# Two panels of a mixer's input product as 512-wide matmuls over high and low parts side by side

## The chip, the core and the metric

The kernel runs on one core of a Trainium2 chip. The metric is the device time of one execution in microseconds. The core has five engines that run their own instruction streams and wait for each other through semaphores: TensorE (PE; its weight loads are listed as PEld), VectorE (DVE), ScalarE (ACT), GpSimd (POOL) and SyncE (SP), which issues the loads here. Matmuls write into PSUM, which has 8 banks of 128 partitions by 512 float32 values; ACT and DVE read them out.

## What is computed

One layer of a hybrid decoder trunk over 256 tokens of width 2048. The part that matters here is the start: a norm, the input product, and the token shift of three of its outputs.

```python
h = rms_norm(x, attn_norm[i])
z = h @ w_in[0]
z_pool = z[..., :POOL_WIDTH]
zs = token_shift(z[..., POOL_WIDTH:IN_WIDTH], mu_shift[i])
...
def token_shift(z, mu):
    zf = z.astype(jnp.float32)
    z_prev = jnp.pad(zf, ((0, 0), (1, 0), (0, 0)))[:, :-1]
    return zf + (z_prev - zf) * mu.astype(jnp.float32)
```

The shifted r, k and v (1024 columns each) feed an RWKV-7 time mixing in two groups of 8 heads; the pooled part feeds a causal pooling; both join in an output product. A squared-ReLU MLP, a gated embedding and a last norm follow.

## The kernel before

Everything is float32, and a product is made of three products of a faster type, float32r. A weight W is split into a high part (an ACT copy into float32r) and a low part (a DVE subtraction), and so is the activation x; W x is taken as Wh xh + Wh xl + Wl xh.

**Stages.** The mixer runs from the start to about 370 us, the MLP after it, then the gate and the last norm. At the start x, transposed, is loaded by k-tile (128 of the 2048 features by 256 tokens), and a small product for the decay, gate and learning-rate inputs runs on it (`wag`). Meanwhile the norm's factor is found. `normed` multiplies each k-tile by it (a DVE product, L438) and splits the result (L176 on ACT, L177 on DVE) into the high tiles `hTh` and the low tiles `hTl`, two tiles each of 8 k-tiles.

**Panels.** The input weights come as panels of 512 columns. `gemm_cols` makes one panel: for each of 8 loads (two k-tiles by 512 columns, split at L171 and L172) and each half of the panel it runs the two column tiles of 128 over both k-tiles, three products of 256 columns each (L184 to L186). The result stands with features on partitions and tokens along the row, two column tiles in one bank, so a panel needs two banks. `z_product` makes such a panel and evacuates each half as soon as it is done: ACT scales it by 1 - mu into SBUF (L487), DVE adds mu times the bank, shifted by a token (L489). The panels are, in order, zk and zr of head group 0, zk and zr of group 1, two of zv, and two of the pooled part, which run in the other orientation.

**Banks.** A ring of three banks (`mm`), one bank apart (`own`) and four for the recurrent work (`rw`) are the 8. zk takes two of the ring, zr one of the ring and `own`, the next zk two of the ring again, so a panel begins in banks that the one before it did not hold.

**Order.** PE's order is written out by hand. The panels are generators in a queue; `fill(us)` runs as many of their steps as their yielded estimates (0.36 us a step) make up, `finish(p)` runs one panel to its end, and between these stand the small products of the recurrent part: the decay and rate products (`rwkv_lora`, L548), the sums and spreads for the key norm (`rwkv_k`, banks `kkn` and `rnb`), the scores (`rwkv_scores`, L640). DVE, ACT, POOL and SP are put in order by a list scheduler with priorities. In `rwkv_k` the keys' norm goes through a root on ACT (L578), a reciprocal (L579) and a spread on PE; DVE then makes the normed keys (L587) and the operands of the scores in tiles `BK` (L606, L607) and `AR` (L608, L611 and, with zr, L616). `make_bands` builds the pooling bands in tile `wband`, on POOL (L133 to L135) and DVE (L136 to L138); this tile takes the place of the norm factor's row, so it waits for the last use of that row in L438.

Of the kernel before, what the change touches and what calls it, by code (L numbers as in the profile page):

```python
# [9 lines left out]
F32 = mybir.dt.float32  # L10
F32R = mybir.dt.float32r
# [5 lines left out]
T = 256  # L17
# [23 lines left out]
def trunk(  # L41
# [43 lines left out]
    def own_bank(name):  # L85
        return psf.tile([128, 512], F32, tag="own", name=name)
# [110 lines left out]
    def gemm_cols(src, acts, name, consume, own=False):  # L197
# [3 lines left out]
        for kp in range(nkp):  # L201
            raw = load_raw(src[kp].rearrange("p a n -> p (a n)"), 1024, f"{name}_{kp}")
            parts = split_w(raw, f"{name}_{kp}")
            for half in range(2):
# [6 lines left out]
                if kp == nkp - 1:  # L211
                    consume(half, banks[half])

    def gemm_toks(src, acts, name, consume, kps=None, hooks=(), banks=None, begin=True, end=True, split_ends=False):
# [54 lines left out]
    def queued(gen):  # L269
        queue.append(gen)  # L270
        return gen
# [5 lines left out]
    def a8(slot, name, dt=F32):  # L277
        return act.tile([128, 2048], dt, tag=f"a{slot}", name=name)
# [27 lines left out]
        nc.vector.reciprocal(rs, rs)  # L306
        return rs

    hT_h = [a8(2 + i, f"hTh{i}", F32R) for i in range(2)]
    hT_l = [a8(4 + i, f"hTl{i}", F32R) for i in range(2)]  # L310

    def hT(k):
        o = (k % 8) * T
        return hT_h[k // 8][:, o : o + T], hT_l[k // 8][:, o : o + T]
# [18 lines left out]
    def flat(t_):  # L333
        return t_.rearrange("p a t -> p (a t)")
# [97 lines left out]
    def normed(*groups):  # L432

        with tc.high_priority(20000):
            xs, hs = [], []
            for k0, n in groups:
                xh = xg[k0 // 4][:, k0 % 4 : k0 % 4 + n]
                nc.vector.tensor_tensor(xh, xh, s_bc.unsqueeze(1).to_broadcast([128, n, T]), op=ALU.mult)  # L438
                xs.append(flat(xh))
                hs.append((k0 // 8, slice(k0 % 8 * T, (k0 % 8 + n) * T)))  # L440
            for x_, (i, o) in zip(xs, hs):
                split_sb(hT_h[i][:, o], hT_l[i][:, o], x_)

    with tc.manual_schedule(engines={mybir.EngineType.DVE}):
        normed((0, 1), (1, 1))
# [25 lines left out]
        nc.scalar.activation(zf[32:64, 2, :], zf[0:32, 2, :], AF.Copy)  # L471


    def z_product(i, tag, mu_name, gi, own):

        box = []

        def consume(half, bank):
            if not box:
                box.append(e4(tag))  # L480
            dst = box[0]
            with tc.high_priority(30000):
                evacs = []
                for p in (2 * half, 2 * half + 1):
                    c = PARAM_COLS[mu_name] - m0 + 4 * gi + p
                    evacs.append((dst[:, p, :], bank[:, p % 2 * T : (p % 2 + 1) * T], col(mu_name, 4 * gi + p)))
                    nc.scalar.activation(evacs[-1][0], evacs[-1][1], AF.Copy, scale=omu[:, c : c + 1])  # L487
                for d_, s_, mu_ in evacs:
                    nc.vector.scalar_tensor_tensor(  # L489
                        d_[:, 1:T], s_[:, 0 : T - 1], mu_, d_[:, 1:T], op0=ALU.mult, op1=ALU.add  # L490
                    )

        return box, queued(gemm_cols(w_in[i + gi], hT, f"{tag}{gi}", consume, own))

    def pair_tile(tag, name, **kw):
# [1133 lines left out]
```

## Time and profile before

| | us |
|---|---|
| median of 3 runs (1162.97 to 1163.73) | 1163.5 |
| the profiled execution | 1163.34 |
| its span | 1161.6 |
| panels zk and zr of group 0 on PE, from the first product to the next panel's | 22.92 to 74.09 |
| first scores product of group 0 | 82.46 |
| clock granted to TensorE, mean | 0.998 |

In the rows of a timeline the first number is the start in microseconds from the start of the span, the second the time covered, then engine, line, operation, output and inputs by the program's names, shapes and count; in square brackets stands how long the engine was idle before it and what it waited for. Matmuls overlap, so the distance between two starts is what one costs, not its duration. The rows of groups give the busy time in us and the mean of one in ns behind the bar.

### The profile page before, as it was taken

What the parts mean: (1) busy time and instruction counts of PE and PEld (TensorE: products, weight loads), DVE (VectorE), ACT (ScalarE), POOL (GpSimd) and SP (SyncE); (2) the same over time, 40 slices, a digit from 0 to 9 for tenths busy, and PEclk for the clock granted to TensorE, in tenths of its full rate; (3) what the DMA queues carried; (4) which work ended last, traced back from release to release, by engine and by line L of the source; (5) the groups of instructions that cost most, each with busy time, mean ns of one, the idle gap of its engine ahead of it and who ended that gap; (6) DMA issues with size and microseconds to landing.
All of it is one profiled execution on the core that took longest, in us unless ns stands there. A gap on an engine that the chain in (4) does not pass through costs nothing.

```text
span 1161.6 us, 19313 instructions
## 1 busy us (share of the span) xinstructions
PE 1150.8 (99%) x7348; PEld 989.2 (85%) x7348; DVE 920.6 (79%) x1223; ACT 689.1 (59%) x1220; POOL 17.2 (1%) x77
## 2 busy tenths in 40 slices
PE   9999999999999999999999999999999999999997
PEld 8999998788888888888888888888888888888886
DVE  7886898356676788888989888888878989888843
ACT  5868555667544655555665755555556665669733
POOL 4100000000000000000000000000000000000000
PEclk9999999999999999999999999999999999999999
DMA  7553544453898999985787887998885778996812
GB/s 274 164 171 127 160 151 152 147 165 109 319 328 277 325 342 343 326 327 191 257 291 250 319 298 280 350 332 328 317 302 180 262 266 287 335 327 227 301 36 73
DMA packets 78445, 290.87 MB, mean 250 GB/s; under 512 B 8720, under 2 KB 9744, under 8 KB 74128
## 3 DMA queue, kind: packets, MB, share of 16 engines
q1 hardware_dynamic: 78064, 289.28, 70.8%
q8 instruction: 57, 0.93, 0.3%
q10 hardware_dynamic: 288, 0.37, 0.1%
q14 instruction: 36, 0.29, 0.1%
HBM read 259.20 MB, written 30.41 MB: 249 GB/s over the span
## 4 chain that ended last, share of the span: by engine, by line
PE 96%; DVE 1%; DMA 1%; ACT 1%; issue 0%; DVEq 0%; ACTq 0%; SPq 0%
PE u_w L1135 21%; PE d_p L1239 15%; PE u_w L1140 10%; PE d_w L1239 9%; PE d_d L1239 3%; PE o_b L193 2%; PE o_b L195 2%; PE o_b L194 2%; PE gt_b L193 2%; PE gt_b L195 2%; PE gt_b L194 2%; PE zp_b L193 2%; PE wag_b L380 1%; PE zr_b L184 1%; PE zk_b L184 1%; PE zk_b L185 1%
## 5 line engine op out<-in xcount | busy, mean ns | idle before, releaser
L1135 PE MATMUL u_w<-h,wh_u 128*128 128x512 f32 x1024 | 321.9, 395 | 0.0
L1140 PEld LDWEIGHTS u_w<-h,wl_u 128*128 128x128 f32 x1024 | 192.4, 188 | 45.4
L171 ACT ACTIVATE wh_u<-raw_u 128x512 fp32r<-128x512 f32 x256 | 147.2, 623 | 133.9 <-PE u_w L1135 99.8
L1140 PE MATMUL u_w<-h,wl_u 128*128 128x256 f32 x1024 | 201.4, 278 | 0.0
L172 DVE TENSOR_TENSOR wl_u<-raw_u,wh_u 128x1024 fp32r<-128x1024 f32 x128 | 156.1, 1220 | 38.1 <-PE u_w L1140 22.6
L1135 PEld LDWEIGHTS u_w<-h,wh_u 128*128 128x128 f32 x1024 | 156.1, 189 | 0.1
L1299 ACT ACTIVATE th_d<-raw_d 128x1024 fp32r<-128x1024 f32 x52 | 52.6, 1053 | 63.1 <-DVE raw_d L1295 43.7
L1239 PE MATMUL d_p<-wh_d,yd 128*128 128x512 f32 x288 | 77.0, 389 | 0.0
L1301 DVE TENSOR_TENSOR tl_d<-raw_d,th_d 128x1024 fp32r<-128x1024 f32 x52 | 61.4, 1221 | 12.4 <-ACT th_d L1299 12.3
L172 DVE TENSOR_TENSOR wl_o<-raw_o,wh_o 128x1024 fp32r<-128x1024 f32 x32 | 39.0, 1223 | 31.3 <-ACT wh_o L171 15.9
L1239 PEld LDWEIGHTS d_p<-wh_d,yd 128*128 128x128 f32 x288 | 54.0, 188 | 11.3
L1239 PE MATMUL d_w<-th_d,ys 128*128 128x512 f32 x240 | 61.5, 390 | 0.0
L171 ACT ACTIVATE wh_o<-raw_o 128x512 fp32r<-128x512 f32 x64 | 36.7, 623 | 40.2 <-PE o_b L194 21.7
L171 ACT ACTIVATE wh_d<-raw_d 128x512 fp32r<-128x512 f32 x96 | 53.9, 619 | 7.0 <-DMA raw_d<-in_w_ffn_down_dram 2.7
L172 DVE TENSOR_TENSOR wl_d<-raw_d,wh_d 128x1024 fp32r<-128x1024 f32 x48 | 57.1, 1217 | 0.0
L1288 ACT ACTIVATE w7h_d<-raw_d 128x1024 fp32r<-128x1024 f32 x40 | 42.2, 1056 | 22.1 <-DMA raw_d<-in_w_ffn_down_dram 8.4
L1239 PEld LDWEIGHTS d_w<-th_d,ys 128*128 128x128 f32 x240 | 44.7, 188 | 9.6 <-ACT th_d L1299 0.5
L1290 DVE TENSOR_TENSOR w7l_d<-raw_d,w7h_d 128x1024 fp32r<-128x1024 f32 x40 | 48.8, 1219 | 4.4 <-PE d_d L1239 2.0
L1239 PE MATMUL d_p<-w7h_d,ys 128*128 128x512 f32 x160 | 49.3, 389 | 0.0
L1239 PE MATMUL d_p<-wl_d,yd 128*128 128x512 f32 x144 | 44.3, 389 | 0.0
L1289 ACT ACTIVATE w7h_d<-raw_d 128x512 fp32r<-128x512 f32 x40 | 25.0, 624 | 24.4 <-PE d_d L1239 19.5
L172 DVE TENSOR_TENSOR wl_zp<-raw_zp,wh_zp 128x1024 fp32r<-128x1024 f32 x16 | 19.5, 1223 | 24.6 <-ACT wh_zp L171 24.6
(390 smaller groups left out, 2694.5 us busy)
## 6 DMA issues: line engine op xcount, KB each, us to landing
raw_u<-in_w_ffn_up_dram SPq DMA_DIRECT2D x128, 512.0 KB, 6.3
raw_d<-in_w_ffn_down_dram SPq DMA_DIRECT2D x106, 512.0 KB, 5.9
raw_ta<-in_w_ffn_down_dram SPq DMA_DIRECT2D x44, 512.0 KB, 6.8
tad<-ta SPq DMA_DIRECT2D x22, 1024.0 KB, 5.7
raw_o<-in_w_out_dram SPq DMA_DIRECT2D x32, 512.0 KB, 5.2
tr_d<-tad SPq DMA_DIRECT2D x28, 512.0 KB, 5.1
raw_gt<-in_w_ple_gate_dram SPq DMA_DIRECT2D x24, 512.0 KB, 4.6
raw_zk<-in_w_in_dram SPq DMA_DIRECT2D x16, 512.0 KB, 3.5
```

The lines of the kernel that those rows point to most:

```text
L171: nc.scalar.activation(wh[:, a * 512 : (a + 1) * 512], raw[:, a * 512 : (a + 1) * 512], AF.Copy)
L172: nc.vector.tensor_tensor(wl, raw, wh.bitcast(F32), op=ALU.subtract)
L193: nc.tensor.matmul(o, a_h, wh[:, 0:n], start=first, stop=False)
L194: nc.tensor.matmul(o, a_l, wh[:, 0:n], start=False, stop=False)
L195: nc.tensor.matmul(o, a_h, wl[:, 0:n], start=False, stop=last)
L1135: nc.tensor.matmul(bank[:, ct, :].rearrange("p (s t) -> p s t", s=2), wh[:, c], hl, start=k == 0, stop=False, skip_group_check=True,)
L1140: nc.tensor.matmul(bank[:, ct, 0:T], wl[:, c], hl[:, 0, :], start=False, stop=k == 15, skip_group_check=True)
L1239: nc.tensor.matmul(o, l, r, start=first, stop=last, skip_group_check=True)
L1288: nc.scalar.activation(ha, ra, AF.Copy)
L1290: nc.vector.tensor_tensor(la, ra, ha.bitcast(F32), op=ALU.subtract)
L1299: nc.scalar.activation(th[:, r], tr[r], AF.Copy)
L1301: nc.vector.tensor_tensor(tl[:, r], tr[r], th[:, r].bitcast(F32), op=ALU.subtract)
```

## The change

The first two panels, zk and zr of head group 0, are made in another way; the six others stay. The high and low part of a normed k-tile now lie side by side in one tile (`hTq`, four tiles of 4 k-tiles each, in the same places), so that one product of the high weights runs over 512 columns: Wh times xh and Wh times xl land in the two halves of a bank. The low weights add their 256 columns onto the first half. A column tile thus fills a bank, and a panel holds four: the whole ring and `own`. Both panels do. To evacuate a tile, ACT copies the second half of the bank, DVE adds the first half to it in a tile `zs`, and the two shift instructions then read `zs` in place of the bank. `zs` lies in the ring of two that the scores' tile uses. A step now covers two column tiles and yields 0.7.

```diff
+    def gemm_cols_wide(src, name, consume):
+        banks = [mm_bank(f"{name}_b{i}") for i in range(3)] + [own_bank(f"{name}_b3")]
...
+            for half in range(2):
+                cts = (2 * half, 2 * half + 1)
+                for a, (wh, wl) in enumerate(parts):
+                    k = 2 * kp + a
+                    hl = hTq[k // 4][:, k % 4]
+                    for ct in cts:
+                        nc.tensor.matmul(
+                            banks[ct].rearrange("p (s t) -> p s t", s=2), wh[:, ct * 128 : (ct + 1) * 128], hl,
+                            start=k == 0, stop=False, skip_group_check=True,
+                        )
+                    for ct in cts:
+                        nc.tensor.matmul(
+                            banks[ct][:, 0:T], wl[:, ct * 128 : (ct + 1) * 128], hl[:, 0],
+                            start=False, stop=k == 2 * nkp - 1, skip_group_check=True,
+                        )
+                    yield 0.7
+                if kp == nkp - 1:
+                    consume(half, [banks[ct] for ct in cts])
...
-    hT_h = [a8(2 + i, f"hTh{i}", F32R) for i in range(2)]
-    hT_l = [a8(4 + i, f"hTl{i}", F32R) for i in range(2)]
+    hTq = [a8(2 + i, f"hT{i}", F32R).rearrange("p (k s t) -> p k s t", k=4, s=2) for i in range(4)]
...
+        def consume_wide(half, banks):
...
+                for p, b in zip(ps, banks):
+                    nc.scalar.activation(zs[:, p], b[:, T : 2 * T], AF.Copy)
+                for p, b in zip(ps, banks):
+                    nc.vector.tensor_tensor(zs[:, p], b[:, 0:T], zs[:, p], op=ALU.add)
+                for p in ps:
+                    nc.scalar.activation(dst[:, p], zs[:, p], AF.Copy, scale=omu[:, c : c + 1])
+                for p in ps:
+                    nc.vector.scalar_tensor_tensor(
+                        dst[:, p, 1:T], zs[:, p, 0 : T - 1], col(mu_name, 4 * gi + p), dst[:, p, 1:T], op0=ALU.mult, op1=ALU.add
+                    )
...
-    zk0, p_zk0 = z_product(4, "zk", "mu_k", 0, False)
-    zr0, p_zr0 = z_product(2, "zr", "mu_r", 0, True)
+    zk0, p_zk0 = z_product(4, "zk", "mu_k", 0, False, True)
+    zr0, p_zr0 = z_product(2, "zr", "mu_r", 0, True, True)
```

The scheduled engines get another order around these panels. First DVE while panel zk ends: the norm's last products and the splits of zk's last loads, then the bands. Of before:

```order
L438 TENSOR_TENSOR tD_t<-tD_t,s_bc 128x512
L339 SCALAR_TENSOR_TENSOR zf<-wagT,par_sb,zf 128x255
L172 TENSOR_TENSOR wl_zk_6_566<-raw_zk_6_563,wh_zk_6_565 128x1024
L177 TENSOR_TENSOR hTl_158<-tD_t,hTh_156 128x512
L438 TENSOR_TENSOR tD_t<-tD_t,s_bc 128x512
L172 TENSOR_TENSOR wl_zk_7_597<-raw_zk_7_594,wh_zk_7_596 128x1024
L177 TENSOR_TENSOR hTl_158<-tD_t,hTh_156 128x512
L136 TENSOR_TENSOR wband<-wband,ident 128x128 x2
```

The same place of the change (its lines lie 25 further down, L463 is the norm product):

```order
L463 TENSOR_TENSOR tD_t<-tD_t,s_bc 128x512
L364 SCALAR_TENSOR_TENSOR zf<-wagT_396,par_sb,zf 32x255
L177 TENSOR_TENSOR hT_158<-tD_t,hT_158 128x2x256
L463 TENSOR_TENSOR tD_t<-tD_t,s_bc 128x512
L172 TENSOR_TENSOR wl_zk_6_520<-raw_zk_6_517,wh_zk_6_519 128x1024
L177 TENSOR_TENSOR hT_158<-tD_t,hT_158 128x2x256
L172 TENSOR_TENSOR wl_zk_7_543<-raw_zk_7_540,wh_zk_7_542 128x1024
L364 SCALAR_TENSOR_TENSOR zf<-wagT,par_sb,zf 128x255
L136 TENSOR_TENSOR wband<-wband,ident 128x128 x2
```

The last norm product moved ahead of the sixth low split. Behind the bands, DVE evacuates zk; there the change has an add for each column tile, `zszk`, ahead of the shifts. Next, DVE from the key norm to the normed keys, of before:

```order
L577 TENSOR_SCALAR rn_860<-kkn 128x32
L594 TENSOR_TENSOR tE_t<-tE_t,zk_t 128x1024
L579 RECIPROCAL rn_860<-rn_860 128x32
L172 TENSOR_TENSOR wl_zr_7_987<-raw_zr_7_984,wh_zr_7_986 128x1024
L580 TENSOR_TENSOR rnq_861<-rn_860,qmask 128x256
L607 TENSOR_TENSOR BK_946<-tE_t,tC_t 128x16x64
L172 TENSOR_TENSOR wl_zk_0_1034<-raw_zk_0_1031,wh_zk_0_1033 128x1024
L587 SCALAR_TENSOR_TENSOR tB_t<-zk_t,par_sb,rnb_928 128x256
```

And of the change, where L623, L625, L640, L626, L653 and L633 are these lines in the same order of work:

```order
L623 TENSOR_SCALAR rn_786<-kkn 128x32
L172 TENSOR_TENSOR wl_zr_7_830<-raw_zr_7_827,wh_zr_7_829 128x1024
L625 RECIPROCAL rn_786<-rn_786 128x32
L640 TENSOR_TENSOR tE_t<-tE_t,zk_t 128x1024
L626 TENSOR_TENSOR rnq_787<-rn_786,qmask 128x256
L172 TENSOR_TENSOR wl_zk_0_928<-raw_zk_0_925,wh_zk_0_927 128x1024
L653 TENSOR_TENSOR BK_856<-tE_t,tC_t 128x16x64
L172 TENSOR_TENSOR wl_zk_1_959<-raw_zk_1_956,wh_zk_1_958 128x1024
L633 SCALAR_TENSOR_TENSOR tB_t<-zk_t,par_sb,rnb_838 128x256
```

zr's last low split now stands ahead of the reciprocal, and the second split of the next panel ahead of the normed keys; on ACT, zr's last high split has moved ahead of the norm's root. Last, DVE from zr's evacuation to the last operand of the scores, of before:

```order
L172 TENSOR_TENSOR wl_zk_1_1065<-raw_zk_1_1062,wh_zk_1_1064 128x1024
L489 SCALAR_TENSOR_TENSOR zr_t<-zr_b_634,par_sb,zr_t 128x255 x2
L489 SCALAR_TENSOR_TENSOR zr_t<-zr_b_635,par_sb,zr_t 128x255 x2
L172 TENSOR_TENSOR wl_zk_2_1096<-raw_zk_2_1093,wh_zk_2_1095 128x1024
L606 TENSOR_TENSOR BK_946<-tF_t,tC_t 128x16x64
L172 TENSOR_TENSOR wl_zk_3_1140<-raw_zk_3_1137,wh_zk_3_1139 128x1024
L611 TENSOR_SCALAR AR_945<-tB_t 128x16
L616 TENSOR_TENSOR AR_945<-zr_t,tA_t 128x16x64
L172 TENSOR_TENSOR wl_zk_4_1183<-raw_zk_4_1180,wh_zk_4_1182 128x1024
```

Of the change, without the first two adds, which stand just before it, and L605's successor between them:

```order
L533 SCALAR_TENSOR_TENSOR zr_t<-zszr_893,par_sb,zr_t 128x255 x2
L528 TENSOR_TENSOR zszr_893<-zr_b_583,zszr_893 128x256
L528 TENSOR_TENSOR zszr_893<-zr_b_584,zszr_893 128x256
L172 TENSOR_TENSOR wl_zk_2_990<-raw_zk_2_987,wh_zk_2_989 128x1024
L533 SCALAR_TENSOR_TENSOR zr_t<-zszr_893,par_sb,zr_t 128x255 x2
L172 TENSOR_TENSOR wl_zk_3_1034<-raw_zk_3_1031,wh_zk_3_1033 128x1024
L652 TENSOR_TENSOR BK_856<-tF_t,tC_t 128x16x64
L172 TENSOR_TENSOR wl_zk_4_1077<-raw_zk_4_1074,wh_zk_4_1076 128x1024
L654 SCALAR_TENSOR_TENSOR AR_855<-tB_t,tA_t 128x16x63
L657 TENSOR_SCALAR AR_855<-tB_t 128x16
L662 TENSOR_TENSOR AR_855<-zr_t,tA_t 128x16x64
```

The adds are new, and zk's fourth low split now stands ahead of the last operand instead of behind it.

More of the change, by code (lines that the diff above doesn't have):

```diff
@@ L212, in gemm_cols @@
                     consume(half, banks[half])
+    def gemm_cols_wide(src, name, consume):
+        banks = [mm_bank(f"{name}_b{i}") for i in range(3)] + [own_bank(f"{name}_b3")]
+        nkp = src.shape[0]
+        for kp in range(nkp):
+            raw = load_raw(src[kp].rearrange("p a n -> p (a n)"), 1024, f"{name}_{kp}")
+            parts = split_w(raw, f"{name}_{kp}")
+            for half in range(2):
[16 more added lines that the diff above has]
+                    consume(half, [banks[ct] for ct in cts])
     def gemm_toks(src, acts, name, consume, kps=None, hooks=(), banks=None, begin=True, end=True, split_ends=False):
@@ L307, in rms_inv @@
         return rs
-    hT_h = [a8(2 + i, f"hTh{i}", F32R) for i in range(2)]
-    hT_l = [a8(4 + i, f"hTl{i}", F32R) for i in range(2)]
+    hTq = [a8(2 + i, f"hT{i}", F32R).rearrange("p (k s t) -> p k s t", k=4, s=2) for i in range(4)]
     def hT(k):
-        o = (k % 8) * T
-        return hT_h[k // 8][:, o : o + T], hT_l[k // 8][:, o : o + T]
+        hl = hTq[k // 4][:, k % 4]
+        return hl[:, 0], hl[:, 1]
     rp = rctx.enter_context(tc.tile_pool(name="rp", bufs=1))
@@ L438, in normed @@
                 nc.vector.tensor_tensor(xh, xh, s_bc.unsqueeze(1).to_broadcast([128, n, T]), op=ALU.mult)
[L439 to L442, printed above, removed]
+                xs.append(xh)
+                hs.append(hTq[k0 // 4][:, k0 % 4 : k0 % 4 + n])
+            for x_, hl in zip(xs, hs):
+                split_sb(hl[:, :, 0], hl[:, :, 1], x_)
     with tc.manual_schedule(engines={mybir.EngineType.DVE}):
@@ L471, in wag_out, with z_product @@
         nc.scalar.activation(zf[32:64, 2, :], zf[0:32, 2, :], AF.Copy)
-    def z_product(i, tag, mu_name, gi, own):
+    def z_product(i, tag, mu_name, gi, own, wide=False):
         box = []
@@ L491, in consume @@
                     )
+        def consume_wide(half, banks):
+            if not box:
+                box.append(e4(tag))
+                box.append(rp.tile([128, 4, T], F32, tag="SC", bufs=2, name=f"zs{tag}{gi}"))
+            dst, zs = box
+            ps = (2 * half, 2 * half + 1)
+            with tc.high_priority(30000):
+                for p, b in zip(ps, banks):
[3 more added lines that the diff above has]
+                for p in ps:
+                    c = PARAM_COLS[mu_name] - m0 + 4 * gi + p
+                    nc.scalar.activation(dst[:, p], zs[:, p], AF.Copy, scale=omu[:, c : c + 1])
[3 more added lines that the diff above has]
+                    )
+        if wide:
+            return box, queued(gemm_cols_wide(w_in[i + gi], f"{tag}{gi}", consume_wide))
         return box, queued(gemm_cols(w_in[i + gi], hT, f"{tag}{gi}", consume, own))
```

## The prediction

> **What bounds the kernel now.** First the page: busy time of each engine, then the chain that ended last. Then the windows over the stage that the change touches (columns: stretch, its length, PE, PEld, DVE, ACT, POOL busy with counts, granted clock, DMA share, GB/s).
>
> ```profile
> PE 1150.8 (99%) x7348; PEld 989.2 (85%) x7348; DVE 920.6 (79%) x1223; ACT 689.1 (59%) x1220; POOL 17.2 (1%) x77
> PE 96%; DVE 1%; DMA 1%; ACT 1%; issue 0%; DVEq 0%; ACTq 0%; SPq 0%
> 54.00:60.00 6.00, 6.00 (x52) 6.00 (x51) 2.50 (x3) 5.97 (x12) 0.00 (x0) 1.00 0.40 119
> 60.00:66.00 6.00, 6.00 (x109) 5.83 (x108) 2.81 (x5) 5.97 (x12) 0.00 (x0) 1.00 0.59 179
> 66.00:72.00 6.00, 6.00 (x53) 5.54 (x53) 6.00 (x9) 2.87 (x7) 0.00 (x0) 1.00 0.49 167
> 72.00:78.00 6.00, 6.00 (x52) 6.00 (x52) 5.97 (x10) 4.17 (x9) 0.00 (x0) 1.00 0.41 124
> 78.00:84.00 6.00, 6.00 (x57) 5.75 (x57) 6.00 (x8) 2.36 (x7) 0.00 (x0) 1.00 0.68 211
> PE zp_b L195 <- DVE wl_zp L172: 0.3, 1, 0.3
> ```
>
> TensorE is the bound: 99% busy, 96% of the chain, clock 1.00. So a shorter instruction stream on PE shortens the kernel, if nobody becomes late. But between 54 and 66 us ACT has 11.94 of 12 us taken, and between 66 and 84 us DVE has 17.97 of 18. The last row, from the list of waits, is PE's only listed wait inside the mixer after its start, 0.3 us near 191 us: hardly anything later could give lost time back.
>
> **What the wide product saves.** Durations of overlapping matmuls say little; the distance between starts counts. The timeline of PE, first inside the old panel zr, then in the MLP's up product, which has the wide form already:
>
> ```profile
> 59.78 0.28 PE L184 MATMUL zr_b<-hTh,wh_zr 128*128 128x256 f32 x1
> ...
> 60.14 0.28 PE L184 MATMUL zr_b<-hTh,wh_zr 128*128 128x256 f32 x1
> 420.19 0.63 PE L1135 MATMUL u_w<-h,wh_u 128*128 128x512 f32 x2
> ...
> 422.28 0.63 PE L1135 MATMUL u_w<-h,wh_u 128*128 128x512 f32 x2
> ```
>
> Old: three products of 256 columns from 59.78 to 60.14, 0.36 us for one k-tile and column tile. New: from 420.19 to 422.28 lie three rounds of two wide and two narrow products, 2.09/6 = 0.348 us. Two panels have 2x16x4 = 128 such pairs: 128 x 0.012 = **1.5 us saved** on PE, half in each panel. That is little, because a step of 256 costs 0.12 us and one of 512 about 0.227: joining two saves only what each start costs over its columns. The Trainium skill (TensorE: Matmul & The Clock Gate, "Back-to-back issue gap") puts that fixed part at 2.5 ns for an isolated product when warm; 128 of them would be an estimate of 0.3 us instead of 1.5. The rows above speak against it here.
>
> **What it adds.** Each of the 8 column tiles gets one ACT copy of the low half and one DVE add before the old two instructions. The nearest rows are the old evacuations, given by groups with operands and shape: the ACT copy out of PSUM, and the DVE product with one operand in PSUM.
>
> ```profile
> L487 ACT ACTIVATE zr_t<-zr_b,omu 128x256 f32<-128x256 f32 x4 | 1.7, 465 | 0.4 <-PE zr_b L186 0.4
> L587 DVE SCALAR_TENSOR_TENSOR tB_t<-zk_t,par_sb,rnb 128x256 f32<-128x256 f32 x4 | 1.6, 473 | 0.0
> ```
>
> Back to back four take about 1.6 us, 0.39 each, so the four adds of a panel are 1.6 us on DVE. They could cost PE nothing, if DVE has room, or 3.2 us, if both panels' adds hit PE; the place decides. There are three places.
>
> **Place A, panel zk to panel zr.** Before, zr had banks of its own. Now it needs zk's four, and each is free only after its add. PE reaches zr at 46.82 - 64x0.012 = 46.05, plus 0.1 for the first k-tile, whose low part must now be there at once: 46.15. The engines there (timeline):
>
> ```profile
> 40.39 0.69 DVE L438 TENSOR_TENSOR tD_t<-tD_t,s_bc 128x512 f32<-128x512 f32 x1
> 41.23 0.38 POOL L133 MEMSET wband<- 128x144 f32 x2 [22.02 <-DVE tD_t L438]
> 44.79 0.38 DVE L136 TENSOR_TENSOR wband<-wband,ident 128x128 f32<-128x128 f32 x1 [0.74 <-POOL wband L135]
> 46.82 0.28 PE L184 MATMUL zr_b<-hTh,wh_zr 128*128 128x256 f32 x1
> 48.75 1.65 DVE L489 SCALAR_TENSOR_TENSOR zk_t<-zk_b,par_sb,zk_t 128x255 f32<-128x255 f32 x4
> 50.15 0.48 PE L548 MATMUL lw<-zf,wa 64*128 64x256 f32 x1
> 51.38 0.82 ACT L551 ACTIVATE tA_t<-lw,par_sb 128x256 f32<-128x256 f32 x2
> ```
>
> Before, DVE came to zk's evacuation only at 48.75, because it built the bands first and waited for POOL, which waited for the last norm product (40.39). Nobody minded. In the new order this product stands before the sixth low split, so POOL starts some 2 to 3 us earlier and its waits on DVE go; the adds then start between 46.1 and 48.75. I take 46.9. First add done at 47.3: PE waits 1.2 us, and 0.5 more for the second bank and the second half: **1.7 us**. Bounds: 0 (adds before 45.7) and 3.2 (first add from 48.75).
>
> Behind this wait stands the lora product (50.15). The fill ahead of it is now 5 units of two pairs, 3.5 us: 46.15+1.7+3.5 = 51.35, and ACT, which read it at 51.38, can start at 51.85. So ACT's full stretch up to 66 us shifts by 0.45.
>
> **Places B and C, panel zk of the second head group, and the scores.** DVE's queue from the key norm to the scores, with PE's arrivals:
>
> ```profile
> 63.41 1.28 ACT L570 ACT_TABLE_LOAD   x1
> 65.79 0.21 ACT L578 ACTIVATE rn<-rn 128x32 f32<-128x32 f32 x1
> 65.91 1.14 ACT L171 ACTIVATE wh_zr<-raw_zr 128x512 fp32r<-128x512 f32 x2
> 65.92 1.23 DVE L594 TENSOR_TENSOR tE_t<-tE_t,zk_t 128x1024 f32<-128x1024 f32 x1 [1.17 <-ACT tE_t L591]
> 67.06 0.35 DVE L579 RECIPROCAL rn<-rn 128x32 f32<-128x32 f32 x1
> 67.33 1.16 DVE L172 TENSOR_TENSOR wl_zr<-raw_zr,wh_zr 128x1024 fp32r<-128x1024 f32 x1
> 68.41 0.41 DVE L580 TENSOR_TENSOR rnq<-rn,qmask 128x256 f32<-128x256 f32 x1
> 68.73 1.22 DVE L607 TENSOR_TENSOR BK<-tE_t,tC_t 128x1024 f32<-128x1024 f32 x1
> 69.87 1.22 DVE L172 TENSOR_TENSOR wl_zk<-raw_zk,wh_zk 128x1024 fp32r<-128x1024 f32 x1
> 71.00 1.65 DVE L587 SCALAR_TENSOR_TENSOR tB_t<-zk_t,par_sb,rnb 128x256 f32<-128x256 f32 x4
> 74.09 0.28 PE L184 MATMUL zk_b<-hTh,wh_zk 128*128 128x256 f32 x1
> 81.14 1.22 DVE L616 TENSOR_TENSOR AR<-zr_t,tA_t 128x1024 f32<-128x1024 f32 x1
> 82.46 0.49 PE L640 MATMUL sc<-AR,BK 64*128 64x128 f32 x4
> ```
>
> The product at L616 ends at 82.36 and the scores start at 82.46: no slack at all. Whatever DVE loses before it, PE loses too. A whole panel-sized operation takes 1.14 us of DVE (68.73 to 69.87). In the new order ACT splits zr's last high part (1.14) ahead of the norm's root, and DVE does its low part, one low split more (zk1) and later another (zk4) ahead of the scores. Worked through: table load at 63.41+0.45 = 63.86, done with the small copy behind it at 65.3; high split to 66.5; DVE from 66.6: low split 1.14, reciprocal 0.27, L594 1.14, L580 0.32, then low split, L607, low split 3.4, so the normed keys (L587) start at 72.9 and the first add at 74.45, done at 74.9.
>
> B: PE reaches zk1 at 74.09 - 1.5 + 0.1 + 1.7 = 74.4, and its first bank is zr's first one: **0.5 us** (0 to 1.5, as A and DVE fall). C: from 74.45 DVE has four adds 1.6, L605 1.1, four shifts 1.6, three low splits and L606 4.6, L608 and L611 1.2, L616 1.2: 11.3, so 85.75, scores at 85.85. PE would be there at 74.9+8.4 = 83.3: **2.5 us** (0 to 3.5).
>
> Sum: -1.5 + 0.1 + 1.7 + 0.5 + 2.5 = **+3.3 us**. The same from one place: scores at 85.85 instead of 82.46. The other edits cost nothing: the norm's outputs written in steps of two k-tiles have the same sizes; zr's ACT copies lie in waits of ACT (it is at 4.17 of 6 us between 72 and 78; without that cover they would add 1.6), zk's before its full stretch begins; the loads keep their sizes, and DMA is at half. The profiled execution took 1163.34 us (span 1161.6 and 1.7 around it), 0.16 under the median of the runs: 1163.34+3.3 = **1166.6**.
>
> **Rivals.**
> *Banks and DVE keep up* (ends on the other side): if the adds find DVE free, only the shorter stream is left: 1163.34 - 1.4 = 1161.9. For it: DVE is busy 5.3 of 12 us between 54 and 66. Against: the scores' zero slack. It decides where L616 ends before 81.1. The Trainium skill (Perfetto Trace Analysis, "Matmuls") has both sides in one place: larger matmuls are more efficient, and independent groups should rotate through different banks so that evacuation overlaps; the first would give this rival, the second is what the change gives up. Chance 0.08.
> *Only the adds count*: ACT gets to the root in time and the splits taken forward hide in DVE's shorter queue behind; L616 is late by zr's four adds alone, 82.36+1.6 = 83.95, scores 1.6 late: 1164.9. For it: ACT's order depends on when buffers come free. Chance 0.22.
> *Place A is full*: DVE still comes at 48.75, A is 3.2, the lora product and ACT are 1.5 later, and all of B and C with them: 1168.1. The same time comes out where the wide products are no faster than three narrow ones. Chance 0.13.
>
> **How the numbers follow.** The forecast has 0.57, its own range 1165.4 to 1167.8. A measurement of this kernel can tell 0.2%, 2.3 us, from no change: slower begins at 1165.8. Slower: most of the forecast, the full place A, a little of the second rival, 0.65; same 0.28; faster 0.07. The range leaves out the first rival and the ends of the bounds: 1162.7 to 1169.0.
>
> **What would show it.** In the new profile: wide and narrow starts 0.347 us a pair; gaps of PE at the first products of zr (sum near 1.7) and of zk1, released by DVE's add; scores starting near 85.8 with PE waiting for DVE's L616 (now L662); DVE without a gap between 66 and 86; from there on every PE row later by one constant. It is wrong if PE has no gap at the panel boundary, if scores start before 82, or if a later stage, such as the wait near 191, swallows the loss.

## The result, and the profile after

| | before | after |
|---|---|---|
| median, us (5 runs each) | 1163.5 (1162.97 to 1163.73) | 1168.3 (1167.43 to 1169.73) |
| the profiled execution, us | 1163.34 | 1167.98 |
| its span, us | 1161.6 | 1166.3 |
| first product of panel zk on PE | 22.92 | 23.43 |
| first scores product of group 0 | 82.46 | 87.00 |

The ratio after to before is 1.0044, 95% interval 1.0033 to 1.0055: 4.8 us slower, by more than the 0.2% that a measurement can tell. One execution each of e7, e11 and e12 below (1.4, 6.5 and 3.3 ms) was disturbed and is left out of the medians; e11's is its profiled one.

The page first: busy time of each engine, then the chain that ended last.

```profile
PE 1149.7 (99%) x7220; PEld 981.6 (84%) x7220; DVE 922.8 (79%) x1231; ACT 692.5 (59%) x1228; POOL 19.2 (2%) x77
PE 92%; DVE 4%; ACT 2%; DMA 1%; issue 1%; SPq 0%; DVEq 0%; ACTq 0%
```

PE has 128 products fewer and is busy 1.1 us less, and yet the span is 4.7 us longer. DVE's share of the chain went from 1% to 4%: PE now waits where it never did. The list of PE's waits names the places (engine, tile and line that waited, what it waited for, us in total, times, longest):

```profile
PE sc L686 <- DVE AR L662: 2.3, 1, 2.3
PE zr_b L227 <- DVE zszk L528: 1.3, 1, 1.3
PE zk_b L184 <- DVE zszr L528: 0.9, 1, 0.9
```

None of the three was in the list of before. They are the prediction's places C, A and B, each released by DVE: the last operand of the scores, zk's add and zr's add. The timeline of PE at these places:

```profile
47.96 0.83 PE L227 MATMUL zr_b<-hT,wh_zr 128*128 128x512 f32 x2 [1.30 <-DVE zszk L528]
...
74.46 0.63 PE L227 MATMUL zr_b<-hT,wh_zr 128*128 128x512 f32 x2
74.93 0.39 PE L232 MATMUL zr_b<-hT,wl_zr 128*128 128x256 f32 x2
76.21 0.39 PE L184 MATMUL zk_b<-hT,wh_zk 128*128 128x256 f32 x1 [0.89 <-DVE zszr L528]
...
84.47 0.28 PE L186 MATMUL zk_b<-hT,wl_zk 128*128 128x256 f32 x1
87.00 0.72 PE L686 MATMUL sc<-AR,BK 64*128 64x128 f32 x8 [2.26 <-DVE AR L662]
```

DVE's queue behind it, where it frees zk's first bank, and then from zr's last low split to the scores:

```profile
46.14 0.29 DVE L138 TENSOR_TENSOR wband<-wband,ident 128x128 f32<-128x128 f32 x1
46.35 1.22 DVE L172 TENSOR_TENSOR wl_zr<-raw_zr,wh_zr 128x1024 fp32r<-128x1024 f32 x1
47.49 0.75 DVE L528 TENSOR_TENSOR zszk<-zk_b,zszk 128x256 f32<-128x256 f32 x2
...
67.95 1.23 DVE L172 TENSOR_TENSOR wl_zr<-raw_zr,wh_zr 128x1024 fp32r<-128x1024 f32 x1 [1.10 <-ACT wh_zr L171]
...
74.17 1.65 DVE L633 SCALAR_TENSOR_TENSOR tB_t<-zk_t,par_sb,rnb 128x256 f32<-128x256 f32 x4
75.74 0.75 DVE L528 TENSOR_TENSOR zszr<-zr_b,zszr 128x256 f32<-128x256 f32 x2
...
85.73 1.22 DVE L662 TENSOR_TENSOR AR<-zr_t,tA_t 128x1024 f32<-128x1024 f32 x1
```

The adds are cheap (two take 0.75, the next instruction starts 0.66 to 0.99 later); what counts is where they stand. ACT had copied the first two banks by 45.84 (its row at 45.18 covers 0.66), 1.65 us before DVE came to them. And the timeline of ACT, its copies of zk's first half and then from the lora product's reader to zr's last high split:

```profile
45.18 0.66 ACT L526 ACTIVATE zszk<-zk_b 128x256 f32<-128x256 f32 x2 [0.35 <-PE zk_b L232]
...
53.32 0.84 ACT L597 ACTIVATE tA_t<-lw,par_sb 128x256 f32<-128x256 f32 x2 [0.78 <-PE la L594]
...
65.37 1.28 ACT L616 ACT_TABLE_LOAD   x1
...
66.78 1.14 ACT L171 ACTIVATE wh_zr<-raw_zr 128x512 fp32r<-128x512 f32 x2
```

The same reader stood at 51.38 before and the table load at 63.41: ACT's stretch is 1.95 us later, and DVE's with it.

**The sum over PE's stream up to the scores.** One narrow step (0.12 us) is taken from each gap. Panel zk: 46.82 - 22.92 = 23.90 before, 46.37 + 0.12 - 23.43 = 23.06 after: -0.84. Gap at zr: 1.585 from start to start, +1.47. Panel zr: 27.27 before, from 47.96 to 75.17 after: -0.06. Gap at zk1: +1.04. zk1 up to the scores: the same within 0.01. Gap at the scores: 2.53 - 0.12 = +2.41. Together 4.0, and 0.51 from zk's later start, 4.54 in all, which is 87.00 - 82.46. The later start is no part of the change: zk's first product stood between 22.66 and 23.54 in ten of the eleven traces below that can be compared, with no order in it (25.07 in the other). From 87 us to the end only 0.1 us is added. So of the 4.64 us between the two profiled executions the change made 4.0, and the rest is mostly this start.

### The profile page after: what moved, and what is told of

The parts are those of the page before. It is cut to its first block, busy times and chain, and to the rows that moved or that the text cites. A ratio compares the mean times of both kernels' runs of the same rounds, so it can differ in the third digit from the quotient of the medians.

```text
span 1166.3 us, 19070 instructions
## 1 busy us (share of the span) xinstructions
PE 1149.7 (99%) x7220; PEld 981.6 (84%) x7220; DVE 922.8 (79%) x1231; ACT 692.5 (59%) x1228; POOL 19.2 (2%) x77
## 4 chain that ended last, share of the span: by engine, by line
PE 92%; DVE 4%; ACT 2%; DMA 1%; issue 1%; SPq 0%; DVEq 0%; ACTq 0%
PE u_w L1181 20%; PE d_p L1285 15%; PE u_w L1186 10%; PE d_w L1285 9%; PE d_d L1285 3%; PE o_b L193 2%; PE o_b L195 2%; PE o_b L194 2%; PE gt_b L193 2%; PE gt_b L194 2%; PE gt_b L195 2%; PE zp_b L193 1%; PE zp_b L195 1%; PE zp_b L194 1%; PE zv_b L184 1%; PE zv_b L186 1%
## 5 line engine op out<-in xcount | busy, mean ns | idle before, releaser
L1347 DVE TENSOR_TENSOR tl_d<-tr_d,th_d 128x1024 fp32r<-128x1024 f32 x28 | 33.0, 1221 | 7.2 <-ACT th_d L1345 7.2
```

The costliest lines, as they stand in the source:

```text
L1347: nc.vector.tensor_tensor(tl[:, r], tr[r], th[:, r].bitcast(F32), op=ALU.subtract)
```

## The experiments

The runs were made in three groups, each with its own runs of the kernel before beside it: medians 1163.38 (1162.74 to 1164.19), 1163.56 (1162.77 to 1165.08) and 1163.30 us (1162.78 to 1164.85). Line numbers in the rows are those of each kernel, up to 5 off those of the change.

| run | what is different | median, us | ratio to before, 95% |
|---|---|---|---|
| e1_layout | both panels narrow, new layout kept | 1163.47 | 0.9994 to 1.0012 |
| e2_wide_zk | only zk wide | 1165.07 | 1.0004 to 1.0022 |
| e3_wide_zr | only zr wide | 1170.72 | 1.0053 to 1.0078 |
| e4_act_frees | ACT frees the banks, adds in SBUF | 1167.64 | 1.0026 to 1.0051 |
| e5_no_add | no copy and add of the low half | 1166.45 | 1.0015 to 1.0034 |
| e6_pool | adds and two products on POOL | 1167.42 | 1.0020 to 1.0043 |
| e7_scores_first | scores' operands ahead of splits | 1169.42 | 1.0033 to 1.0061 |
| e8_filled | e3, with products in its two pauses | 1168.45 | 1.0031 to 1.0056 |
| e9_bands_later | bands behind zk's evacuation | 1169.21 | 1.0034 to 1.0060 |
| e10_zk_bands | only zk wide, bands later | 1164.08 | 0.9996 to 1.0014 |
| e11_narrow4 | four banks, three narrow products | 1171.42 | 1.0049 to 1.0077 |
| e12_before_bands | before, bands later | 1163.72 | 0.9994 to 1.0012 |

### The layout alone, and one panel at a time

```diff
-    zk0, p_zk0 = z_product(4, "zk", "mu_k", 0, False, True)
-    zr0, p_zr0 = z_product(2, "zr", "mu_r", 0, True, True)
+    zk0, p_zk0 = z_product(4, "zk", "mu_k", 0, False)          # e1, e3
+    zr0, p_zr0 = z_product(2, "zr", "mu_r", 0, True)           # e1, e2
```

> Only the new layout of the normed x (four tiles of high and low parts by k-tile); both panels as before, narrow. DVE-queue theory: the layout costs nothing, 1163.5 us (1163.1 to 1164.0), scores at 82.5. Rival, the layout itself costs (writes in steps of two k-tiles, or the later first product, 23.43 instead of 22.92): 0.5 us or more above before, up to the whole 4.8.

> Only zk wide, zr narrow as before. DVE-queue theory: 0.75 us saved on PE, the bank wait at the first products of zr stays (about 1.5 to 2 us in all, since zr's two banks are two of zk's four), no wait at the next panel, scores about 1 us late: 1164.6 us (1164.0 to 1165.4). Rival, a wide panel is slower in itself, each by the same amount: half of the loss, 1165.9.

> Only zr wide, zk narrow as before. DVE-queue theory: no wait at zr's start, but DVE's queue from 66 us to the scores has the same four adds and the same splits taken forward, so the scores stand near 86 again and nearly the whole loss is here without place A: 1167.3 us (1166.4 to 1168.2). Rival, a wide panel is slower in itself: 1165.9. Rival, the hand-over of banks from zk to zr is the cause: 1163.0 or less.

The layout costs nothing that can be told (1163.47 beside 1163.38). zk alone costs 1.7 us, within the expected range, and its wait is place A alone (its list of waits):

```profile
PE zr_b L184 <- DVE zszk L528: 1.7, 2, 1.3
```

zr alone was a miss: 7.3 us over before, more than both panels together. Its list of waits shows why PE stands longer, and the windows around the first wait something that nobody had expected (the next to last columns: granted clock, DMA share, GB/s):

```profile
PE zr_b L227 <- DVE zk_t L514: 2.5, 1, 2.5
PE sc L686 <- DVE AR L662: 2.3, 1, 2.3
```

```profile
49.00:50.00 1.00, 0.38 (x2) 0.37 (x3) 1.00 (x4) 0.00 (x0) 0.00 (x0) 0.96 0.77 221
50.00:51.00 1.00, 1.00 (x5) 0.90 (x4) 1.00 (x2) 0.00 (x0) 0.00 (x0) 0.50 0.74 242
...
52.00:53.00 1.00, 1.00 (x5) 0.85 (x4) 0.00 (x0) 0.00 (x0) 0.00 (x0) 0.50 0.69 135
53.00:54.00 1.00, 1.00 (x6) 0.85 (x6) 0.00 (x0) 0.23 (x1) 0.00 (x0) 0.83 0.75 287
```

First, the narrow zk is evacuated in before's order, at 48.61 behind the bands and two low splits, and zr's second bank is one of zk's: this is the rival "place A is full", and the gap is 2.92 us from start to start. Second, after the pause the granted clock is 0.50 for 0.08 + 3.00 + 0.34 = 3.42 us (the shortfalls of the windows' clock, doubled), which costs half of that, 1.71 us. The same happens after its pause ahead of the scores, again for 3.42 us. Two pauses, two falls of the clock: about 3.4 us on top of the waits in this execution (1172.22). It is the slowest of the five, and how many falls the others had no trace shows.

### Is the lower clock a price of the pause?

```diff
         banks = [mm_bank(f"{name}_b{i}") for i in range(3)] + [own_bank(f"{name}_b3")]
+        for _ in range(10):
+            nc.tensor.matmul(banks[0], hTq[0][:, 0, 0, 0:128], hTq[0][:, 0].rearrange("p s t -> p (s t)"), start=True, stop=True)
...
             bks = [rw_bank(f"sc{e}") for e in range(2)]
+            if gi == 0 and c == 0:
+                for _ in range(9):
+                    nc.tensor.matmul(bks[0], hTq[0][:, 0, 0, 0:128], hTq[0][:, 0].rearrange("p s t -> p (s t)"), start=True, stop=True)
```

> The kernel with only zr wide (1170.7 us, 2.4 us over the change) with products whose result is overwritten put into its two long waits: 10 of 512 columns (2.3 us) ahead of zr's first product, 9 (2.0 us) ahead of the scores, each into a bank that the next product starts afresh. They lie inside waits of 2.9 and 2.5 us, so that work waits no longer than before. Theory (after a pause of 2.5 us the granted clock falls to 0.50 for 3.5 to 3.9 us, as that kernel's trace shows from 49.9 and from 90.9 us, and each costs half its length, 1.8 to 1.9 us): granted clock 1.00 throughout, 1167 to 1168. Rival (the lower clock is chance or costs nothing, the length of the waits is all): 1170 to 1171.

It took 1168.45, 2.3 us less than e3, for 19 products more. That is a little above the expected 1167 to 1168, and far from the rival's 1170 to 1171. Its windows over the same stretch:

```profile
49.00:50.00 1.00, 0.75 (x4) 0.36 (x3) 1.00 (x4) 0.00 (x0) 0.00 (x0) 1.00 0.72 234
50.00:51.00 1.00, 1.00 (x8) 0.91 (x7) 1.00 (x2) 0.00 (x0) 0.00 (x0) 1.00 0.82 242
...
52.00:53.00 1.00, 1.00 (x7) 0.80 (x5) 0.00 (x0) 0.78 (x2) 0.00 (x0) 1.00 0.57 119
```

zr's second product starts at 49.63 against 49.62: the wait ends at the same moment, but PE was not idle in it, and the clock stays at 1.00. The scores start at 87.89 instead of 89.43. So the lower clock is a price of the pause: 3.41 us long, where the expectation had read 3.5 to 3.9.

### The adds, the banks and DVE's queue

```diff
-                    nc.scalar.activation(zs[:, p], b[:, T : 2 * T], AF.Copy)
+                    nc.scalar.activation(zz[:, :, p], b.rearrange("p (s t) -> p s t", s=2), AF.Copy)        # e4, e6
...
-                    nc.vector.tensor_tensor(zs[:, p], b[:, 0:T], zs[:, p], op=ALU.add)
+                    nc.vector.tensor_tensor(zs[:, p], zs[:, p], zl[:, p], op=ALU.add)                       # e4
+                    nc.gpsimd.tensor_tensor(zs[:, p], zs[:, p], zl[:, p], op=ALU.add)                       # e6
...
-                    nc.scalar.activation(dst[:, p], zs[:, p], AF.Copy, scale=omu[:, c : c + 1])
+                    nc.scalar.activation(dst[:, p], b[:, 0:T], AF.Copy, scale=omu[:, c : c + 1])            # e5, without the two lines above
...
-        nc.vector.tensor_tensor(k2, k2, zk, op=ALU.mult)
+        (nc.vector if gi else nc.gpsimd).tensor_tensor(k2, k2, zk, op=ALU.mult)                             # e6, and BK's second slot likewise
```

> Both panels wide, but ACT copies a whole bank (512 columns) into SBUF and DVE adds the halves there, so that a bank is free after ACT alone; DVE has the same number of instructions. Theory that the scores' operands on DVE set the loss: the waits at the first products of zr and of zk1 shrink (below 1 us together), the one before the scores grows by as much, 1167.8 us (1167.0 to 1168.6). Rival, the banks held by DVE's adds set it: those 2.2 to 3 us come off, 1165.3.

> The changed kernel without the copy and the add of the low half: ACT and DVE evacuate the first half of each bank as before, so Wh times xl is left out of zk and zr. Eight adds (0.33 us each on DVE by the changed kernel's trace, 2.6 us) and eight copies go; PE's stream and the banks stay. Theory (the banks are handed over through DVE's queue, and the adds lengthen that queue): the gap at zr's first product shrinks by one or two adds only, to 0.8 to 1.3 us, and the wait ahead of the scores by zr's four adds and what zk's cost, to about 1 us; 1165.5 to 1166.3. Rival (the adds are the whole loss): no gaps, the shorter stream alone is left, 1162 to 1162.5. Rival (the adds cost nothing, order and banks all): 1168, as the change.

> The changed kernel with ACT copying both halves of a bank into SBUF, the eight adds on POOL, and the two products of group 0 that need zk (k2 and the second slot of BK, 1.14 us each on DVE) on POOL as well. DVE loses 4.9 us of work ahead of the scores, POOL was busy 2% of the time. Theory (DVE's amount of work ahead of the scores is what they wait for): the wait ahead of the scores goes, what is left at zr's first products is the wait for ACT's copies, 1.3 us or less, less 1.5 us of shorter stream: 1163 to 1164. Rival (the wait ahead of the scores hangs on ACT's later key norm, not on DVE's work): scores still 1 to 2 us late, 1165 to 1166. Rival (POOL's adds are slow, several us each, and shift_evac waits for them): 1168 or more.

The list of waits of e4, where ACT frees the banks:

```profile
PE sc L687 <- DVE AR L663: 2.1, 1, 2.1
PE zr_b L227 <- ACT zszk L527: 1.3, 1, 1.3
PE zk_b L186 <- DVE wl_zk L172: 0.9, 1, 0.9
```

The list has three waits of nearly the same size, but two of them stand elsewhere. By e4's timeline zr now starts at 46.08 without a wait, and the 1.3 us stand at its second half (48.96): ACT's copies of zk's second half start at 48.33, behind its scaled copy of the first half (47.52), which waits for DVE's add at 47.07 (ACT's timeline):

```profile
47.52 0.91 ACT L532 ACTIVATE zk_t<-zszk,omu 128x256 f32<-128x256 f32 x2 [1.66 <-DVE zszk L529]
```

So DVE's queue still sets A, through ACT. B is gone: zk1 starts at 74.52, at once behind zr. PE waits 0.9 us instead at 81.56, for the third low split of zk1. The time is in the theory's range; the wait ahead of the scores did not grow as the theory had expected; it fell by 0.2 us. Of e5, where Wh times xl is left out of zk and zr and nothing is copied or added:

```profile
PE zr_b L227 <- DVE zk_t L528: 1.4, 1, 1.4
PE sc L681 <- DVE AR L657: 1.1, 1, 1.1
PE zk_b L184 <- DVE zr_t L528: 0.9, 1, 0.9
```

The adds are worth 1168.3 - 1166.45 = 1.9 us, 1.2 of it in the wait ahead of the scores (2.3 to 1.1). 2.9 us of loss is left without a single add: A and B are the hand-over of the banks in DVE's queue, as the theory had it. It expected A a little smaller than it came, and the time 0.15 us lower at most.

e6 was a miss. The wait ahead of the scores went, and one of 2.8 us for a low split of zk1 came in its place; behind that one the clock fell too (from 83.15 on), which is 1.71 us of the profiled execution's loss. Its timeline of DVE, and then of POOL, shows what happened:

```profile
67.97 2.30 DVE L627 TENSOR_TENSOR rnq<-rn,qmask 128x256 f32<-128x256 f32 x1
70.19 5.08 DVE L172 TENSOR_TENSOR wl_zk<-raw_zk,wh_zk 128x1024 fp32r<-128x1024 f32 x2
75.20 1.64 DVE L634 SCALAR_TENSOR_TENSOR tB_t<-zk_t,par_sb,rnb 128x256 f32<-128x256 f32 x4
```

```profile
67.59 2.39 POOL L641 TENSOR_TENSOR tE_t<-tE_t,zk_t 128x1024 f32<-128x1024 f32 x1 [17.62 <-ACT tE_t L638]
70.06 2.45 POOL L654 TENSOR_TENSOR BK<-tE_t,tC_t 128x1024 f32<-128x1024 f32 x1
73.03 2.84 POOL L529 TENSOR_TENSOR zszr<-zszr 128x256 f32<-128x256 f32 x2 [0.52 <-ACT zszr L527]
```

While POOL works, DVE's products of two SBUF tensors take 2.30 instead of 0.41 and about 2.5 instead of 1.2, so that DVE loses 4.5 us between 67.97 and 75.2 (2.30 + 5.08 instead of 0.41 + 2 x 1.23) to be spared 4.9. The normed keys, with one operand in PSUM, take their usual 1.64, and their first two lie beside POOL's add, which ends at 75.87. The Trainium skill (SBUF — State Buffer, "Who interferes with whom") states this: a DVE instruction with two SBUF inputs contends with a GpSimd instruction that reads SBUF, for ports that are locked exclusively, and outside the two-port modes one with at most one SBUF input doesn't. The rows agree: the product at 67.97 ends at 70.27, 0.28 us behind the end of POOL's at 69.98, and the two low splits, taken singly, end at 73.59 and 75.27, each 1.08 us behind the end of a POOL instruction.

### Is it the order in DVE's queue, or its length?

```diff
+        with tc.high_priority(25000):
-        nc.vector.tensor_tensor(k2, k2, zk, op=ALU.mult)
+            nc.vector.tensor_tensor(k2, k2, zk, op=ALU.mult)
...
-        nc.vector.tensor_tensor(slot(BK, r_slot[gi]), v3(k2), v3(EI), op=ALU.mult)
+            nc.vector.tensor_tensor(slot(BK, r_slot[gi]), v3(k2), v3(EI), op=ALU.mult)
```

AR's products stand in such a block too.

> The changed kernel with DVE's operands of the scores (key products, BK, AR) at a higher priority than the low splits of the next panel, so that the order in DVE's queue changes and nothing else. Theory (there is too much DVE work ahead of the scores, whatever its order, since PE needs the low splits of zk1 as well): the scores come early, the wait stands at zk1's low products instead, 1167 to 1169.5. Rival (two low splits moved ahead of the scores' operands are the cause, as the order suggests): the wait falls by 1.1 to 2.3 us, 1165.7 to 1167.

It took 1169.42, in the theory's range. The wait ahead of the scores is gone from the list, and the same wait stands at zk1:

```profile
PE zk_b L186 <- DVE wl_zk L172: 2.1, 1, 2.1
```

```profile
81.68:85.10 3.42, 1.35 (x11) 1.14 (x10) 3.42 (x5) 1.15 (x2) 0.00 (x0) 1.00 0.12 47
85.10:88.51 3.41, 3.41 (x18) 3.19 (x18) 3.13 (x6) 0.00 (x0) 0.00 (x0) 0.50 0.89 264
```

DVE has more to do between the key norm and the scores than PE leaves it time for; order only chooses who waits. The second view, the windows around this pause and behind it, shows the clock at half again. Less the 1.71 us of this fall, the profiled execution of 1169.69 would be at 1167.98, where that of the change is.

### Place A without the bands, and what it does further on

```diff
-    def make_bands():
+    def make_bands(after):
         wband = mc.tile([128, 4, 272], F32, tag="wband", name="wband")
+        nc.gpsimd.tensor_copy(wband[:, :, 0:1], after[:, :, 0:1])
...
-    wband = make_bands()
+    wband = make_bands(zk0[0])
```

> The changed kernel with the pooling bands made to wait for zk's evacuation (a small copy of zk into the band tile ahead of them), so that DVE's nine band operations no longer stand ahead of the first add; nothing else. By the changed kernel's trace the first add stood at 47.49, behind the bands and two low splits, while its bank and ACT's copy were there at about 45.8. Theory (place A is DVE's queue order, and its wait goes on through the lora product, ACT and DVE to the scores): gap at zr's first product 0.3 to 0.8 us instead of 1.6, the lora product and ACT's chain about 1 us earlier, the scores about 1 us earlier: 1166.5 to 1167.3. Rival (the scores' lateness is DVE's own work, A is absorbed there): scores as late as before, 1168. Rival (bands now collide behind with the key norm): 1168.5 or more.

> Only zk wide (1165.1 us so far), zr as before, and the bands waiting for zk's evacuation as in the run beside it. Theory: of its gaps (1.6 and 0.7 us at zr's first products, by its trace) most goes, and 0.75 us of shorter stream in one panel stays: 1163 to 1164. Rival (the gap is the hand-over of the banks whatever DVE's order): 1165.

> Control: the kernel before, with the bands waiting for zk's evacuation. It has no gap at zr's first product that this could close, so 1163.3 to 1163.8 if later bands harm nothing; 1164.5 or more if they push the key norm or the scores' operands back, in which case the two runs with later bands carry that cost too.

The timeline of e9, DVE, ACT and PE in turn:

```profile
45.51 0.75 DVE L529 TENSOR_TENSOR zszk<-zk_b,zszk 128x256 f32<-128x256 f32 x2
```

```profile
51.91 0.84 ACT L598 ACTIVATE tA_t<-lw,par_sb 128x256 f32<-128x256 f32 x2 [0.79 <-PE la L595]
...
63.96 1.28 ACT L617 ACT_TABLE_LOAD   x1
```

```profile
46.01 0.81 PE L228 MATMUL zr_b<-hT,wh_zr 128*128 128x512 f32 x2
...
85.58 0.70 PE L687 MATMUL sc<-AR,BK 64*128 64x128 f32 x6 [2.25 <-DVE AR L663]
```

The adds stand 2 us earlier, zr starts with no wait (its second half waits 0.6), ACT's reader and table load are 1.41 us earlier, and so are the scores (1.42; 0.48 of it is zk's earlier start). The mechanism is as expected, and yet the median is 1169.21, no better than the change. The windows around the scores' pause and behind it show what the profiled execution lost again:

```profile
82.53:85.95 3.42, 1.17 (x13) 0.97 (x13) 3.42 (x6) 0.00 (x0) 0.00 (x0) 1.00 0.92 331
85.95:89.36 3.41, 3.41 (x24) 3.19 (x22) 2.46 (x6) 2.75 (x6) 0.00 (x0) 0.50 0.07 26
```

The clock was at half for 3.41 us here, 1.71 us lost, where the change's own profiled execution had 1.00 behind an equal pause. The fastest run of e9, 1166.73 at a mean clock of 0.998, lies in the expected 1166.5 to 1167.3; its profiled one, 1169.21, has 0.996 and would be at 1167.50 without this fall. Another 0.9 us of its lead went later, most of it in the MLP near 1012 us, where its list has a wait that the change's hasn't (PE d_w for ACT th_d, 0.6 us). The median also lies in the range of the rival that the bands collide with the key norm, but the trace doesn't show that: ACT, DVE and the scores all come earlier. The other three runs (1168.94 to 1170.35) have no trace, so that they lost by the clock too isn't shown; two of them took over a microsecond more than the profiled one, which this fall doesn't explain. What the later bands are worth in the change itself stays open.

With zk alone wide, where no pause is longer than 1.3 us, later bands bring 1.0 us (1165.07 to 1164.08); that is just above the expected 1163 to 1164. In the kernel before, later bands do nothing that can be told (1163.72 beside 1163.30). So the best wide version is as fast as before, not faster.

### Taking the 512-wide product away

In e11 each half of a bank gets a product of its own, both with the start flag on the first k-tile; the kernel leaves part of the sum out of zk and zr.

```diff
-                            banks[ct].rearrange("p (s t) -> p s t", s=2), wh[:, ct * 128 : (ct + 1) * 128], hl,
+                            banks[ct][:, s * T : (s + 1) * T], wh[:, ct * 128 : (ct + 1) * 128], hl[:, s],   # for s in range(2)
```

> The changed kernel with its banks and its evacuation, but Wh times xh and Wh times xl as two products of 256 columns into the two halves of the bank instead of one of 512. It takes the faster product away and leaves the rest. Theory (the scores wait for DVE, so what PE gains ahead of them only lengthens its wait): 1168 to 1169.2, with smaller gaps at zr, zk1 and the scores. Rival (the wide product saves its 1.5 us also here): 1169.6 to 1170.2. Rival (the first wide product after an interruption costs so much that nothing is saved): 1168 or less, and the same gaps.

It took 1171.42, outside all three ranges, and settles nothing. The scheduler put DVE into another order (the sixth low split of zk ahead of the last norm product again, as in before), so that place A changed as well; its mean granted clock was only 0.995 or 0.996; and no usable trace shows the gaps. What the wide product alone brings inside the change stays open.

## Why the prediction came out as it did

The forecast was 1166.6, slower, in a range of 1162.7 to 1169.0; the kernel took 1168.3. The three places, their order and what releases PE at each were right, and so was the statement that nothing later gives the time back (0.1 us from the scores to the end). By its steps, against the +3.3 us of its sum:

- **The shorter stream, -1.5 and +0.1.** A pair costs 0.347 to 0.348 as predicted, and zk came out at -0.84. In zr only 0.06 was left. 0.19 is the wait of its second half, which the prediction had put into A. About 0.4 was mis-sized: eight wide products of zr take 0.33 to 0.34 us to the next start instead of 0.23, the first two of each half (in the rows above, the pair at 47.96 covers 0.83 and the one at 74.46 0.63) and the first behind each of four groups of small products. Before, a first product cost more only behind these four groups, 0.223 instead of 0.120. That is 0.8 us against 0.4.
- **Place A, 1.7.** 1.47 at the first product and 0.19 at the second half: the right size. The adds start at 47.49, 0.1 later than foreseen once zk's start is taken out (46.9 + 0.51). e9 shows that the bands ahead of the add are most of the cause: without them it starts at 45.51, zr starts without a wait, and 0.6 us are left at its second half.
- **ACT's stretch, +0.45.** This step failed: 1.95 with zk's later start, 1.44 without. The lora product's first start was taken at 51.35 and its reader at 51.85; but the reader needs all of these products (its wait in the row above names the last one), and came 1.23 us behind the first of them before (50.15 to 51.38) and 1.17 after (52.15 to 53.32).
- **Place B, 0.5.** 1.04, because DVE carries ACT's delay: zr's first add at 75.74, not 74.45.
- **Place C, 2.5.** 2.41. DVE's last operand started 1.2 us later than worked out, but PE came 1.3 later as well, so that the difference was right and the moment was not (87.00, not 85.85). That two errors of this size cancel is luck in part. An add costs 0.33 us, not 0.39.
- **The other edits, nothing:** right for the layout, by e1.
- **DVE without a gap from 66 to 86:** right from 67.95 to 89.7, but not from 66: ahead of 67.95 it stood 0.9 and 1.1 us, first for the sums of the key norm on PE and then for zr's last high split on ACT.
- **The rival "only the adds count"** (1.6 us in all for zr's adds): e5 puts all eight at 1.9 us of 4.8. They are a part of it, the banks and the queue the larger one.
- **The rival "place A is full"** came nearest in number (1168.1), not in its cause: A was 1.7, not 3.2. Its other condition, wide products no faster than three narrow ones, came near to true in zr, where 0.06 us was saved, and not in zk.
- **The rival "banks and DVE keep up":** the best that could be made of it, e10, is level with before.

What the prediction did not have at all is the granted clock. It took 1.00 as given, and every wait at its own length. A pause of over 2 us can cost 1.71 us more, by where it falls (see the end). In the change's profiled execution it did not; two of its five runs had a mean clock of 0.996 against 0.998 and took 1169.61 and 1169.73, the other three 1167.43 to 1168.30. That fits one fall of the clock ahead of or behind the scores, but no trace of those two runs shows it.

## What to carry to other kernels

Before a product is made wider, look at what frees its banks: four banks instead of two turn a panel boundary into a wait for another engine's queue, and 0.012 us a pair is soon lost there. Where that queue is full and the next product depends on its last entry, an instruction added to it is paid nearly in full (zr's four adds take 1.3 us, and the wait ahead of the scores is 1.2 shorter without the adds), whatever the order, and another engine helps only if it doesn't slow the first. Price a wait not by its length alone: over 2 us it may bring a slower clock behind it.

## What the hardware showed that was not expected

**The clock behind a pause.** The list of waits holds seven pauses of PE between 2.1 and 2.8 us in the traces of the change, e3 (two), e4, e6, e7 and e9. Behind five of them the granted clock fell to 0.50, 0.3 to 1.5 us after work began again, each time for 3.41 us; behind those of the change and of e4 it did not. Behind pauses of up to 1.4 us it never did. The clock records also show which pauses are followed by a fall. In one trace the falls begin a whole number of 3.413 us apart: in e3 at 49.92, 90.88 and 1166.08, the last one behind the end of PE's work, and the distances are 12 and 315 times 3.413. Every trace that can be compared has such a last fall, and it gives the grid of its execution. Here are the windows on this grid at the scores' pause: two of the change, the one of e3 ahead of its fall, and two of e4 with the 0.9 us wait ahead of it (length, then PE's busy time; the clock is the third number from the end):

```profile
82.67:86.09 3.42, 2.08 (x18) 1.87 (x16) 3.30 (x5) 0.68 (x2) 0.00 (x0) 1.00 0.83 274
86.09:89.50 3.41, 2.50 (x27) 2.38 (x28) 3.41 (x7) 1.96 (x6) 0.00 (x0) 1.00 0.44 143
87.47:90.88 3.41, 1.45 (x19) 1.33 (x20) 3.41 (x8) 0.92 (x4) 0.00 (x0) 1.00 0.74 258
81.60:85.01 3.41, 2.49 (x19) 2.29 (x19) 3.41 (x5) 0.00 (x0) 0.00 (x0) 1.00 0.70 217
85.01:88.43 3.42, 2.26 (x25) 2.14 (x26) 3.42 (x7) 1.72 (x6) 0.00 (x0) 1.00 0.75 242
```

In the window ahead of each of the five falls PE was idle for 1.96 to 2.77 us (e3 above: 3.41 - 1.45). In no other window before the end of the work was it idle for more than 1.34 us. A border of the grid cuts the change's pause into 1.34 and 0.91, and the one of e4 so that its windows have 0.92 and 1.16 us of idle time; nearly the same pause lies within one window in e9 (82.53 to 85.95, above). So where a pause falls on the grid decides, and the grid lies differently in every execution: its first border stands between 0.2 and 3.2 us from the start in the traces. Between 1.34 and 1.96 us no trace shows what happens. The Trainium skill (TensorE: Matmul & The Clock Gate, Part 1) speaks of a free-running window of about 3.4 us, and the traces agree. Its advice to allow no gap over about 3 us ("Why this matters for your kernels") is too generous by these rows: 1.96 us within one window was enough in e3.

**The first product after an interruption** takes 0.10 us more to the next start: a narrow one behind small products 0.223 instead of 0.120 (before), a wide one 0.337 instead of 0.233 (the change).

**DVE beside POOL:** products of two SBUF tensors took 2.1 to 5.6 times their time while POOL read SBUF (e6; the two low splits are taken together).
